# GpSimd's loads and normalisations in one pinned order, in a masked-patch loss on one core

## The chip, the core and the metric

The kernel runs on one core of a Trainium2 chip. The metric is the device time of one execution in microseconds (us), lower is better. The kernel before took 97.32 us in the median of three runs (97.21 to 97.70). The engines are called TensorE (PE, with its weight loads PEld), VectorE (DVE), ScalarE (ACT), GpSimd (POOL) and SyncE (SP), as in the profile.

## The reference

`pred` and `target` are float32 arrays of 32 x 147 x 768 (196 patches, three quarters of them masked). Each row of 768 values of the target is normalised, the squared difference to the prediction is averaged over the row, and the 147 rows of each batch entry are averaged.

```python
mean = target.mean(axis=-1, keepdims=True)
var = target.var(axis=-1, keepdims=True)
target = (target - mean) / np.sqrt(var + 1e-6)
loss = np.mean((pred - target) ** 2, axis=-1)
return loss.mean(axis=-1).astype(np.float32)
```

## The kernel before

The 4,704 rows are laid over 128 partitions: a batch entry has four partitions, and each of these has 37 rows of 768 values, save that the fourth has 36. So there are 36 full columns k = 0 to 35 of 128 rows, and a rest column 36 of 96 rows. Each tensor is loaded in pieces of columns. The target has a rest piece, whose tile is called t36, and nine pieces of four columns, t0, t4, ... t32 (the number is the first column). The prediction has p36, then p0, p4, ... p28 of four columns, and then p32 of two columns, p34 and p35 of one. All of them are loaded by GpSimd's DMA queue (line 66), which turns the float32 of the memory into bfloat16 on the way; a piece of four columns is 768 KB in the core's memory. Every piece has a buffer of its own, so no load waits for room. A load's issue does wait for something else: the loads take turns at eight completion semaphores, and a load is issued only when the eighth load ahead of it has landed.

For each target piece, `stats` takes mean and variance of each row on VectorE: two `bn_stats` of 384 values (line 116) and a `bn_aggr` (line 117) per column. ScalarE takes the square root for the piece (line 118, from `mv` to `r`), VectorE the reciprocal (line 120) and `nmr`, which is minus mean times `r`, by a `scalar_tensor_tensor` (line 121).

For each prediction piece, `losses` goes over its columns. GpSimd makes the normalised column `s` = t * r + nmr in bfloat16 (line 142, 128 x 768 each, 37 in all). TensorE forms pred - s in a PSUM tile `z` by four matmuls with the identity and minus the identity (line 147: `s` with 512 and 256 columns, then `p` with 512 and 256; I call these four a tile of TensorE's work). There are three `z` buffers. ScalarE squares `z` and sums it over the row (line 149, an ACTIVATE and an ACTIVATION_READ_ACCUMULATOR; "a Square" below is the pair). When all columns of a piece are squared, a small matmul adds the sums `rl` of the piece to `acc`, weighted by a mask (line 153, two of them in the trace). At the end VectorE adds four columns of `acc` (line 167), and SyncE writes 32 numbers out.

Each engine works through its own instructions in a fixed order. A scheduler sets that order when the kernel is built, from the code and its dependencies. On GpSimd it puts all 22 loads ahead of the first normalised column. `work`, the pool of `s`, has 6 buffers, and so has `small`, the pool of `r`, `nmr`, `mv`, `st` and `rl`.

Of the kernel before, what the change touches and what calls it, by code (L numbers as in the profile page):

```python
# [8 lines left out]
BF16 = mybir.dt.bfloat16  # L9
ALU = mybir.AluOpType  # L10
# [4 lines left out]
def kernel(  # L15
# [7 lines left out]
    nc = tc.nc  # L23
    B, N, D = pred.shape
    eps = 1e-6
    P = 128
    J = P // B
    KJ = (N + J - 1) // J
    KM = N - (J - 1) * KJ
    assert KJ == KM + 1  # L30
    RP = B * (J - 1)
# [6 lines left out]
    def main_rows(x, k0, k1):  # L38
        return bass.AP(tensor=x.tensor, offset=x.offset + k0 * D,
                       ap=[[N * D, B], [KJ * D, J], [1, (k1 - k0) * D]])  # L40

    def rest_rows(x):
        return bass.AP(tensor=x.tensor, offset=x.offset + KM * D,
                       ap=[[N * D, B], [KJ * D, J - 1], [1, D]])

    data = ctx.enter_context(tc.tile_pool(name="data", bufs=1))
    work = ctx.enter_context(tc.tile_pool(name="work", bufs=6))
    small = ctx.enter_context(tc.tile_pool(name="small", bufs=6))
    singles = ctx.enter_context(tc.tile_pool(name="singles", bufs=1))
    psum = ctx.enter_context(tc.tile_pool(name="psum", bufs=3, space=bass.MemoryType.PSUM))  # L50
# [3 lines left out]
    t_pieces = [None] + [(k, k + 4) for k in range(0, KM, 4)]  # L54
    p_pieces = [None] + [(k, k + 4) for k in range(0, KM - 4, 4)] + [(KM - 4, KM - 2), (KM - 2, KM - 1), (KM - 1, KM)]

    tbuf, pbuf = {}, {}

    def load(kind, piece):
        x = targ_f if kind == "t" else pred_f  # L60
        k0, k1 = piece if piece else (KM, KM + 1)
        rows = P if piece else RP
        dt = BF16 if kind == "t" else BF16
        til = data.tile([P, (k1 - k0) * D], dt, name=f"{kind}{k0}")
        eng = nc.gpsimd if kind == "t" else nc.gpsimd
        eng.dma_start(out=til[:rows], in_=main_rows(x, k0, k1) if piece else rest_rows(x))  # L66
        for k in range(k0, k1):
            (tbuf if kind == "t" else pbuf)[k] = (til, (k - k0) * D, rows)

    eps_t = singles.tile([P, 1], F32)  # L70
    nc.vector.memset(eps_t, eps)  # L71

    load("t", t_pieces[0])
    load("t", t_pieces[1])
    load("p", p_pieces[0])
    load("t", t_pieces[2])

    ident = singles.tile([P, P], BF16)
    nident = singles.tile([P, P], BF16)
# [12 lines left out]
        masks[name] = m  # L92

    seq = []
    for i in range(3, len(t_pieces)):
        seq += [("p", p_pieces[i - 2]), ("t", t_pieces[i])]
    seq += [("p", q) for q in p_pieces[len(t_pieces) - 2:]]
    for kind, piece in seq:
        load(kind, piece)

    acc = psum1.tile([B, 4], F32)
    rs = {}

    def stats(piece):
        k0, k1 = piece if piece else (KM, KM + 1)
        rows = P if piece else RP
        K = k1 - k0
        r = small.tile([P, K], F32, name="r")
        nmr = small.tile([P, K], F32, name="nmr")
        if norm_pix_loss:  # L110
            mv = small.tile([P, K, 2], F32, name="mv")
            for k in range(k0, k1):
                til, o, _ = tbuf[k]
                st = small.tile([P, 2, 6], F32, name="st")
                for j in range(2):
                    nc.vector.bn_stats(out=st[:rows, j, :], in_=til[:rows, o + j * half:o + (j + 1) * half])  # L116
                nc.vector.bn_aggr(out=mv[:rows, k - k0], in_=st[:rows])  # L117
            nc.scalar.activation(out=r[:rows], in_=mv[:rows, :, 1], func=ACTF.Sqrt,  # L118
                                 bias=eps_t[:rows], scale=1.0)
            nc.vector.reciprocal(out=r[:rows], in_=r[:rows])  # L120
            nc.vector.scalar_tensor_tensor(out=nmr[:rows], in0=mv[:rows, :, 0], scalar=-1.0,  # L121
                                           in1=r[:rows], op0=ALU.mult, op1=ALU.mult)
        else:
            nc.vector.memset(r, 1.0)
            nc.vector.memset(nmr, 0.0)
        for k in range(k0, k1):
            rs[k] = (r[:rows, k - k0:k - k0 + 1], nmr[:rows, k - k0:k - k0 + 1])

    n_acc = [0]
    total_acc = len(p_pieces)  # L130

    def losses(piece):
        k0, k1 = piece if piece else (KM, KM + 1)
        rows = P if piece else RP
        K = k1 - k0
        rl = small.tile([P, 4], F32, name="rl")
        for k in range(k0, k1):
            r, nmr = rs[k]
            til, o, _ = tbuf[k]
            ptil, po, _ = pbuf[k]  # L140
            s = work.tile([P, D], BF16, name="s")
            nc.gpsimd.tensor_scalar(out=s[:rows], in0=til[:rows, o:o + D], scalar1=r, scalar2=nmr,  # L142
                                    op0=ALU.mult, op1=ALU.add)
            z = psum.tile([P, 2 * BANK], F32, name="z")
            for src, so, w, first in ((s, 0, nident, True), (ptil, po, ident, False)):
                for c0, c1 in ((0, BANK), (BANK, D)):
                    nc.tensor.matmul(z[:rows, c0:c1], w[:rows, :rows], src[:rows, so + c0:so + c1],  # L147
                                     start=first, stop=not first)
            nc.scalar.activation(out=z[:rows, :D], in_=z[:rows, :D], func=ACTF.Square,  # L149
                                 accum_out=rl[:rows, k - k0:k - k0 + 1])  # L150
        if K < 4:
            nc.vector.memset(rl[:, K:], 0.0)
        nc.tensor.matmul(acc, masks["main" if piece else "rest"][:rows], rl[:rows],  # L153
                         start=n_acc[0] == 0, stop=n_acc[0] == total_acc - 1)
        n_acc[0] += 1

    done_p = 0
    cols = [p[1] if p else 0 for p in t_pieces]
    for i, tp in enumerate(t_pieces):
        stats(tp)  # L160
        hi = cols[i]
        while done_p < len(p_pieces) and (p_pieces[done_p] is None or p_pieces[done_p][1] <= hi):
            losses(p_pieces[done_p])
            done_p += 1

    ob = singles.tile([B, 1], F32)
    nc.vector.tensor_reduce(out=ob, in_=acc, axis=mybir.AxisListType.X, op=ALU.add)  # L167
# [36 lines left out]
```

## Time and profile before

| what | us |
|---|---|
| median of three runs | 97.32 |
| the profiled execution, its own time | 97.15 |
| its span, first to last instruction | 95.4 |
| GpSimd busy | 49.6 |
| VectorE busy | 43.9 |
| ScalarE busy | 36.1 |
| TensorE matmuls busy | 33.4 |

The profiled execution's time is 1.75 us longer than its span. The granted TensorE clock is 0.997. Rows of the timeline give the start, the duration, the engine, the line, the operation with output and inputs, the count of instructions merged in the row, and in brackets how long the engine was idle before and what ended the wait. Rows of 40 slices have one digit per fortieth of the span (2.39 us), the busy share in tenths.

### The profile page before, as it was taken

Reading aid. Unit: us, or ns where it says so; the run is one execution under the profiler, and the core shown is the slowest. Engines: PE = TensorE matmul, PEld = TensorE weight load, DVE = VectorE, ACT = ScalarE, POOL = GpSimd, SP = SyncE. Lnnn points to the kernel's source line nnn. Section 1 sums busy time; section 2 is a strip of 40 time slices with the busy share of each in tenths; the row PEclk is TensorE's granted clock in tenths of the full one; section 3 lists DMA queues with packets and bytes.
Section 4 is the critical chain, followed back from the end, with each engine's and each line's share of the span. In section 5 each row is a group of like instructions: output and inputs, shape, how many; then the busy total and the mean of one; then the engine's idle time right before and its main releaser. Section 6 shows DMA issues by size and latency. Waiting matters only on the chain.

```text
span 95.4 us, 762 instructions
## 1 busy us (share of the span) xinstructions
PE 33.4 (35%) x172; PEld 16.4 (17%) x172; DVE 43.9 (46%) x137; ACT 36.1 (38%) x85; POOL 49.6 (52%) x73
## 2 busy tenths in 40 slices
PE   0000000000000000000003999999897894388800
PEld 0000000000000000000002355444343442143400
DVE  0044989549439529629519609609980000100000
ACT  5010010100100100100001379999998999099910
POOL 5996220220220210211209999999999990899400
PEclk9999999999999999999999999999999999999998
DMA  0899999999999999999999999999990000000000
GB/s 0 142 211 211 211 214 214 211 211 214 221 217 209 214 216 216 219 211 211 219 216 214 211 211 219 219 212 211 204 165 0 0 0 0 0 0 0 0 0 0
DMA packets 3156, 14.49 MB, mean 152 GB/s; under 512 B 400, under 2 KB 848, under 8 KB 3152
## 3 DMA queue, kind: packets, MB, share of 16 engines
q0 software_dynamic: 3104, 14.45, 74.7%
q8 instruction: 1, 0.02, 0.1%
q14 instruction: 3, 0.02, 0.1%
q1 hardware_dynamic: 48, 0.00, 0.0%
HBM read 28.90 MB, written 0.00 MB: 303 GB/s over the span
## 4 chain that ended last, share of the span: by engine, by line
DMA 65%; ACT 15%; DVE 7%; issue 3%; POOL 3%; PE 2%; ACTq 0%; POOLq 0%
DMA t<-in_target_dram 65%; ACT z L149 14%; DVE st L116 4%; DVE nmr L121 3%; POOL s L142 2%; PE z L147 2%; POOL t L66 1%; DVE mv L117 1%; ACTq L149 0%; DVE r L120 0%; PE acc L153 0%; ACT r L118 0%; DVE ob L167 0%; POOLq L142 0%; ACTq L199 0%
## 5 line engine op out<-in xcount | busy, mean ns | idle before, releaser
L116 DVE BATCH_NORM_STATS2 st<-t 128x6 f32<-128x384 bf16 (+1 forms) x74 | 36.4, 531 | 25.2 <-DMA t<-in_target_dram 25.2
L147 PE MATMUL z<-s,nident 128*128 128x512 bf16 (+1 forms) x74 | 19.5, 347 | 56.2 <-POOL s L142 56.1
L142 POOL TENSOR_SCALAR s<-t,r,nmr 128x768 bf16<-128x768 bf16 (+1 forms) x37 | 35.8, 982 | 3.0 <-DVE r L120 2.9
L149 ACT ACTIVATE z<-z 128x768 f32<-128x768 f32 (+1 forms) x37 | 29.4, 794 | 5.0 <-PE z L147 3.9
L118 ACT ACTIVATE r<-mv,eps_t 128x4 f32<-128x4 f32 (+1 forms) x10 | 2.9, 295 | 49.2 <-DVE mv L117 35.8
L147 PE MATMUL z<-p,ident 128*128 128x512 bf16 (+1 forms) x74 | 19.7, 347 | 0.0
L66 POOL DMA_DIRECT2D p<-in_pred_dram x12 | 6.8, 566 | 22.4 <-DMA p<-in_pred_dram 16.2
L147 PEld LDWEIGHTS <-nident 128*128 128x128 bf16 (+1 forms) x74 | 7.2, 103 | 63.8 <-issue 54.3
L66 POOL DMA_DIRECT2D t<-in_target_dram x10 | 5.8, 584 | 14.0 <-DMA t<-in_target_dram 13.1
L147 PEld LDWEIGHTS <-ident 128*128 128x128 bf16 (+1 forms) x74 | 7.6, 103 | 5.6 <-issue 1.2
L117 DVE BATCH_NORM_AGGREGATE mv<-st 128x2 f32<-128x12 f32 (+1 forms) x37 | 7.3, 196 | 0.3
L149 ACT ACTIVATION_READ_ACCUMULATOR z<-z 128x1 f32 (+1 forms) x37 | 7.0, 190 | 0.0
L120 DVE RECIPROCAL r<-r 128x4 f32<-128x4 f32 (+1 forms) x10 | 1.7, 170 | 11.2 <-ACT r L118 11.2
L167 DVE TENSOR_REDUCE ob<-acc 32x1 f32<-32x4 f32 x1 | 0.1, 150 | 9.9 <-PE acc L153 9.9
L121 DVE SCALAR_TENSOR_TENSOR nmr<-mv,r 128x4 f32<-128x4 f32 (+1 forms) x10 | 3.7, 372 | 0.2
L153 PE MATMUL acc<-rl,mask_main 128*32 128x4 f32 x22 | 2.4, 183 | 1.8 <-ACT z L149 1.8
L153 PEld LDWEIGHTS acc<-rl,mask_main 128*32 128x32 f32 x22 | 1.5, 108 | 4.9 <-ACT z L149 3.3
L118 ACT ACT_TABLE_LOAD x1 | 1.3, 1283 | 0.8 <-PEq L185 0.8
L71 DVE MEMSET eps_t<- 128x1 f32 x1 | 0.1, 59 | 0.9 <-PEq L185 0.9
L82 POOL TENSOR_SCALAR_AFFINE_SELECT ident<-ident 128x128 bf16<-128x128 bf16 x1 | 0.4, 390 | 0.0
L82 POOL TENSOR_SCALAR_AFFINE_SELECT nident<-nident 128x128 bf16<-128x128 bf16 x1 | 0.4, 388 | 0.0
L90 POOL TENSOR_SCALAR_AFFINE_SELECT mask_main<-mask_main 128x32 f32<-128x32 f32 x1 | 0.3, 337 | 0.0
(14 smaller groups left out, 3.1 us busy)
## 6 DMA issues: line engine op xcount, KB each, us to landing
t<-in_target_dram POOLq DMA_DIRECT2D x9, 768.0 KB, 26.3
p<-in_pred_dram POOLq DMA_DIRECT2D x8, 768.0 KB, 29.0
p<-in_pred_dram POOLq DMA_DIRECT2D x1, 384.0 KB, 27.2
p<-in_pred_dram POOLq DMA_DIRECT2D x2, 192.0 KB, 23.1
t<-in_target_dram POOLq DMA_DIRECT2D x1, 144.0 KB, 3.2
p<-in_pred_dram POOLq DMA_DIRECT2D x1, 144.0 KB, 6.8
out_dram<-ob SPq DMA_DIRECT2D x1, 0.1 KB, 2.9
```

The lines of the kernel that those rows point to most:

```text
L66: eng.dma_start(out=til[:rows], in_=main_rows(x, k0, k1) if piece else rest_rows(x))
L82: nc.gpsimd.affine_select(out=til, in_=til, compare_op=ALU.not_equal, fill=v, base=0, pattern=[[-1, P]], channel_multiplier=1)
L90: nc.gpsimd.affine_select(out=m[:rows], in_=m[:rows], compare_op=ALU.is_ge, fill=0.0, base=per - 1, pattern=[[per, B]], channel_multiplier=-1)
L116: nc.vector.bn_stats(out=st[:rows, j, :], in_=til[:rows, o + j * half:o + (j + 1) * half])
L117: nc.vector.bn_aggr(out=mv[:rows, k - k0], in_=st[:rows])
L118: nc.scalar.activation(out=r[:rows], in_=mv[:rows, :, 1], func=ACTF.Sqrt, bias=eps_t[:rows], scale=1.0)
L120: nc.vector.reciprocal(out=r[:rows], in_=r[:rows])
L121: nc.vector.scalar_tensor_tensor(out=nmr[:rows], in0=mv[:rows, :, 0], scalar=-1.0, in1=r[:rows], op0=ALU.mult, op1=ALU.mult)
L142: nc.gpsimd.tensor_scalar(out=s[:rows], in0=til[:rows, o:o + D], scalar1=r, scalar2=nmr, op0=ALU.mult, op1=ALU.add)
L147: nc.tensor.matmul(z[:rows, c0:c1], w[:rows, :rows], src[:rows, so + c0:so + c1], start=first, stop=not first)
L149: nc.scalar.activation(out=z[:rows, :D], in_=z[:rows, :D], func=ACTF.Square, accum_out=rl[:rows, k - k0:k - k0 + 1])
L153: nc.tensor.matmul(acc, masks["main" if piece else "rest"][:rows], rl[:rows], start=n_acc[0] == 0, stop=n_acc[0] == total_acc - 1)
```

## The change

Normalising is taken out of `losses` into a function of its own, which writes `s` for all columns of a target piece as soon as their statistics are there, and which issues one load after the first column and one after the fourth. Loads and normalised columns carry a mark by which the scheduler keeps them in the order of the code. Three target pieces of four columns, not two, are loaded ahead of the first prediction piece of four columns, so each target piece from t8 on comes one place earlier among the loads and the prediction pieces p24 and p28 follow each other after t32. Eight loads come ahead of the first normalised column. The `work` pool has 20 buffers instead of 6. The last target piece gets its statistics and its normalised columns in two groups of two columns. `losses` of a prediction piece is now written after the normalising of the next target piece.

```diff
-    work = ctx.enter_context(tc.tile_pool(name="work", bufs=6))
+    work = ctx.enter_context(tc.tile_pool(name="work", bufs=20))
...
+    pin = tc.keep_in_program_order
...
-        eng.dma_start(out=til[:rows], in_=main_rows(x, k0, k1) if piece else rest_rows(x))
+        pin(eng.dma_start(out=til[:rows], in_=main_rows(x, k0, k1) if piece else rest_rows(x)))
...
     load("t", t_pieces[2])
+    load("t", t_pieces[3])
...
-    for i in range(3, len(t_pieces)):
-        seq += [("p", p_pieces[i - 2]), ("t", t_pieces[i])]
-    seq += [("p", q) for q in p_pieces[len(t_pieces) - 2:]]
-    for kind, piece in seq:
-        load(kind, piece)
+    for i in range(4, len(t_pieces)):
+        seq += [("p", p_pieces[i - 3]), ("t", t_pieces[i])]
+    seq += [("p", q) for q in p_pieces[len(t_pieces) - 3:]]
+    todo = iter(seq)
+
+    def load_next():
+        nxt = next(todo, None)
+        if nxt is not None:
+            load(*nxt)
+
+    for _ in range(3):
+        load_next()
...
+    sbuf = {}
+
+    def normalise(piece):
+        k0, k1 = piece if piece else (KM, KM + 1)
+        rows = P if piece else RP
+        for k in range(k0, k1):
+            r, nmr = rs[k]
+            til, o, _ = tbuf[k]
+            s = work.tile([P, D], BF16, name="s")
+            pin(nc.gpsimd.tensor_scalar(out=s[:rows], in0=til[:rows, o:o + D], scalar1=r, scalar2=nmr,
+                                        op0=ALU.mult, op1=ALU.add))
+            sbuf[k] = s
+            if k == k0 or k == k0 + 3:
+                load_next()
...
-            r, nmr = rs[k]
-            til, o, _ = tbuf[k]
+            s = sbuf[k]
             ptil, po, _ = pbuf[k]
-            s = work.tile([P, D], BF16, name="s")
-            nc.gpsimd.tensor_scalar(out=s[:rows], in0=til[:rows, o:o + D], scalar1=r, scalar2=nmr,
-                                    op0=ALU.mult, op1=ALU.add)
...
-    done_p = 0
-    cols = [p[1] if p else 0 for p in t_pieces]
-    for i, tp in enumerate(t_pieces):
-        stats(tp)
-        hi = cols[i]
-        while done_p < len(p_pieces) and (p_pieces[done_p] is None or p_pieces[done_p][1] <= hi):
-            losses(p_pieces[done_p])
-            done_p += 1
+    stats(t_pieces[0])
+    normalise(t_pieces[0])
+    for i, tp in enumerate(t_pieces[1:]):
+        k0, k1 = tp
+        groups = [tp] if i < len(t_pieces) - 2 else [(k0, k0 + 2), (k0 + 2, k1)]
+        for g in groups:
+            stats(g)
+            normalise(g)
+        losses(p_pieces[i])
+    for pp in p_pieces[len(t_pieces) - 1:]:
+        losses(pp)
```

The order of instructions shows what this moves. In the lists below a tile's name is followed by a number of its own (t4_81 is the tile t4), L66 and L67 are the loads, L142 and L147 on GpSimd are the normalised columns.

GpSimd before, its last six loads and the first columns:

```order
L66 DMA p24_125<-in_pred_dram 128x1x3072
L66 DMA t32_127<-in_target_dram 128x1x3072
L66 DMA p28_129<-in_pred_dram 128x1x3072
L66 DMA p32_131<-in_pred_dram 128x1x1536
L66 DMA p34_133<-in_pred_dram 128x1x768
L66 DMA p35_135<-in_pred_dram 128x1x768
L142 TENSOR_SCALAR s_149<-t36_75,r_138,nmr_139 96x768
L142 TENSOR_SCALAR s_182<-t0_77,r_159,nmr_160 128x768
```

GpSimd now, from the last of the eight loads that stand ahead of normalising:

```order
L67 DMA p4_107<-in_pred_dram 128x1x3072
L147 TENSOR_SCALAR s_120<-t36_75,r_110,nmr_111 96x768
L67 DMA t16_122<-in_target_dram 128x1x3072
L147 TENSOR_SCALAR s_146<-t0_77,r_124,nmr_125 128x768
L67 DMA p8_148<-in_pred_dram 128x1x3072
L147 TENSOR_SCALAR s_150<-t0_77,r_124,nmr_125 128x768
L147 TENSOR_SCALAR s_152<-t0_77,r_124,nmr_125 128x768
L147 TENSOR_SCALAR s_154<-t0_77,r_124,nmr_125 128x768
L67 DMA t20_156<-in_target_dram 128x1x3072
L147 TENSOR_SCALAR s_189<-t4_81,r_167,nmr_168 128x768
L67 DMA p12_191<-in_pred_dram 128x1x3072
```

Fourteen loads now stand behind one or more normalised columns; the last, p35, stands behind the first column of t24, and the load of t32 behind the fourth column of t12.

ScalarE before, around the square roots of the last two target pieces (L118 is a square root, L149 a Square; r_607 belongs to t32, z_520 to z_544 to p24, z_576 on to p28):

```order
L149 ACTIVATE z_528,rl_517<-z_528 128x768
L149 ACTIVATE z_536,rl_517<-z_536 128x768
L149 ACTIVATE z_544,rl_517<-z_544 128x768
L118 ACTIVATE r_551<-mv_553,eps_t_73 128x4
L118 ACTIVATE r_607<-mv_609,eps_t_73 128x4
L149 ACTIVATE z_576,rl_573<-z_576 128x768
```

ScalarE now, around the same roots (L127 is a square root, L169 a Square; r_525 belongs to t28, r_581 and r_599 to the two halves of t32, z_442 to z_460 to p16, z_500 is the first of p20):

```order
L127 ACTIVATE r_525<-mv_527,eps_t_73 128x4
L169 ACTIVATE z_442,rl_441<-z_442 128x768
L127 ACTIVATE r_581<-mv_583,eps_t_73 128x2
L169 ACTIVATE z_448,rl_441<-z_448 128x768
L169 ACTIVATE z_454,rl_441<-z_454 128x768
L169 ACTIVATE z_460,rl_441<-z_460 128x768
L127 ACTIVATE r_599<-mv_601,eps_t_73 128x2
L169 ACTIVATE z_500,rl_499<-z_500 128x768
```

Behind the root of t32 there stood 8 Squares; now 19 stand behind the root of its first half, and the last 16 of these, p20 to p35, behind the root of the second.

TensorE before, at the end of piece p20 (the rows of z_488 are the end of its fourth tile, those of z_520 the start of p24's first; the accumulating matmul of p20 comes only after two tiles of p24):

```order
L147 MATMUL z_488<-p20_121,ident_83 128x512
L147 LDWEIGHTS ident_83
L147 MATMUL z_488<-p20_121,ident_83 128x256
L147 LDWEIGHTS nident_84
L147 MATMUL z_520<-s_518,nident_84 128x512
```

TensorE now, at the end of piece p16 and the start of p20:

```order
L167 MATMUL z_460<-p16_251,ident_85 128x512
L167 LDWEIGHTS ident_85
L167 MATMUL z_460<-p16_251,ident_85 128x256
L173 MATMUL acc_109<-rl_441,mask_main_95 32x4
L167 LDWEIGHTS nident_86
L167 MATMUL z_500<-s_429,nident_86 128x512
```

The accumulating matmul of p16 now stands ahead of p20's first tile; that of p20 stands behind one tile of p24, that of p24 inside the second tile of p28, and that of p28 behind the two tiles of p32.

## The prediction

> **What bounds the kernel now.** I read the page's slices first, for where the time lies, then the timelines of GpSimd, ScalarE, VectorE and TensorE around the points where they wait. The page: the span and the slices of GpSimd and of the transfers.
>
> ```profile
> span 95.4 us, 762 instructions
> ...
> POOL 5996220220220210211209999999999990899400
> ...
> DMA  0899999999999999999999999999990000000000
> ```
>
> The transfers run without a gap through slice 30, that is to 71.6 us (30 x 95.4 / 40). GpSimd does next to nothing until the middle of the span and is then busy to the end. Its timeline says what it does there:
>
> ```profile
> 42.68 0.53 POOL L66 DMA_DIRECT2D p<-in_pred_dram  x1 [3.12 <-DMA t<-in_target_dram]
> 46.38 0.53 POOL L66 DMA_DIRECT2D p<-in_pred_dram  x1 [3.17 <-DMA p<-in_pred_dram]
> 50.00 0.53 POOL L66 DMA_DIRECT2D p<-in_pred_dram  x1 [3.10 <-DMA t<-in_target_dram]
> 50.57 20.27 POOL L142 TENSOR_SCALAR s<-t,r,nmr 96x768 bf16<-96x768 bf16 x21
> 71.05 7.74 POOL L142 TENSOR_SCALAR s<-t,r,nmr 128x768 bf16<-128x768 bf16 x8 [0.21 <-DVE r L120]
> 81.50 7.74 POOL L142 TENSOR_SCALAR s<-t,r,nmr 128x768 bf16<-128x768 bf16 x8 [2.71 <-DVE r L120]
> ```
>
> Each load waits about 3.1 us for an earlier one to land, and all 37 normalised columns stand behind the last load. So the first column starts at 50.57; 37 columns at 0.968 us (7.74 / 8) are 35.8 us, with 2.9 us of waits they end at 89.24. The timeline of ScalarE shows that it follows this pace:
>
> ```profile
> 55.44 0.30 ACT L118 ACTIVATE r<-mv,eps_t 128x4 f32<-128x4 f32 x1 [1.46 <-POOL s L142]
> 55.65 0.79 ACT L149 ACTIVATE z<-z 128x768 f32<-128x768 f32 x1
> ...
> 56.46 0.79 ACT L149 ACTIVATE z<-z 128x768 f32<-128x768 f32 x1
> ...
> 67.07 0.79 ACT L149 ACTIVATE z<-z 128x768 f32<-128x768 f32 x1
> ...
> 79.75 0.80 ACT L149 ACTIVATE z<-z 128x768 f32<-128x768 f32 x1
> 80.46 0.19 ACT L149 ACTIVATION_READ_ACCUMULATOR z<-z 128x1 f32 x1
> ...
> 83.45 0.80 ACT L149 ACTIVATE z<-z 128x768 f32<-128x768 f32 x1 [2.42 <-PE z L147]
> ...
> 90.20 0.80 ACT L149 ACTIVATE z<-z 128x768 f32<-128x768 f32 x1
> ```
>
> From 83.45 to 90.20 seven Squares take 0.964 us each: GpSimd's pace. From 56.46 to 67.07, with a stock of columns ready, thirteen take 0.816 us each: ScalarE's own pace. The last ACTIVATE ends at 91.00; 4.4 us later the span ends.
>
> **The loads move, the transfers should not.** GpSimd is now asked, per target piece, for 4 columns (3.87 us) and 2 issues (1.06 us), 4.93 us in all. The target pieces come as these rows of VectorE's timeline show, each the first statistics of a piece (t12, t28, t32), then the ends of t32's second and fourth aggregation and the `nmr` that follows:
>
> ```profile
> 27.78 1.48 DVE L116 BATCH_NORM_STATS2 st<-t 128x6 f32<-128x384 bf16 x3 [2.36 <-DMA t<-in_target_dram]
> ...
> 57.08 1.48 DVE L116 BATCH_NORM_STATS2 st<-t 128x6 f32<-128x384 bf16 x3 [3.10 <-DMA t<-in_target_dram]
> ...
> 64.40 1.48 DVE L116 BATCH_NORM_STATS2 st<-t 128x6 f32<-128x384 bf16 x3 [3.09 <-DMA t<-in_target_dram]
> ...
> 66.79 0.19 DVE L117 BATCH_NORM_AGGREGATE mv<-st 128x2 f32<-128x12 f32 x1
> ...
> 68.43 0.21 DVE L117 BATCH_NORM_AGGREGATE mv<-st 128x2 f32<-128x12 f32 x1
> 68.56 2.30 DVE L121 SCALAR_TENSOR_TENSOR nmr<-mv,r 128x4 f32<-128x4 f32 x1
> ```
>
> One period is 7.32 us, of two pieces of 3.66 us, so GpSimd has 2.4 us to spare in each. Each load issue now stands behind columns that wait for statistics. The load of t32 stands behind the fourth column of t12. t12 now comes one place earlier, at 24.1 (27.78 - 3.66); its statistics take 4.24 us (68.43 + 0.21 - 64.40), root and `nmr` another 0.5 or so, four columns and the issue between them 4.4: the load is issued at about 33.3, and t32's transfer can begin at 57.1, one piece ahead of its landing. The cover is 24 us, and the same count for p35, behind t24's first column, leaves about 18. So I cost the move at nothing for the transfers, with an end at 71.6 as before. Were the cover gone, every us of late issue would be a us of late end. That transfers slow down because GpSimd now normalises beside them is bounded by two stretches of the trace, without columns and with them, and by the last one, which holds the end of the data:
>
> ```profile
> 30.00:50.00 20.00, 0.00 (x0) 0.00 (x0) 11.32 (x36) 0.59 (x2) 2.64 (x5) 1.00 1.04 214
> 50.60:64.00 13.40, 12.38 (x58) 5.93 (x58) 7.54 (x23) 9.76 (x25) 13.40 (x14) 1.00 1.04 214
> 64.00:71.00 7.00, 6.09 (x33) 3.07 (x34) 6.56 (x16) 6.81 (x17) 6.84 (x8) 1.00 1.04 206
> ```
>
> The last figure is GB/s: 214 in both. I take no slowing; the far end is 206, 3.7% less, which would bring t32 2.2 us later.
>
> **What is late next.** With t28's columns done by about 62 (it comes at 53.4, 4.24 for statistics, 0.5, 3.9), GpSimd no longer holds anybody. The order on ScalarE does: 19 Squares stand behind the root of t32's first half, and 16 of them behind that of the second. These 16 (p20 to p35) would take 13.1 us at 0.816, and none may start before t32 has come, although p20 and its columns are there long before. The timelines of TensorE and of ScalarE have the rows that price the start of this run:
>
> ```profile
> 51.61 0.80 PE L147 MATMUL z<-s,nident 96*96 96x512 bf16 x2 [51.61 <-POOL s L142]
> ...
> 55.71 0.85 PE L147 MATMUL z<-s,nident 128*128 128x512 bf16 x2
> ...
> 56.99 0.61 PE L147 MATMUL z<-s,nident 128*128 128x512 bf16 x2
> ...
> 58.09 0.49 PE L147 MATMUL z<-p,ident 128*128 128x512 bf16 x2
> ...
> 58.74 0.49 PE L147 MATMUL z<-p,ident 128*128 128x512 bf16 x2
> ...
> 80.71 0.23 PE L153 MATMUL acc<-rl,mask_main 128*32 128x4 f32 x2 [1.05 <-ACT z L149]
> ...
> 82.54 0.48 PE L147 MATMUL z<-s,nident 128*128 128x512 bf16 x2 [1.61 <-POOL s L142]
> ```
>
> ```profile
> 53.08 0.79 ACT L149 ACTIVATE z<-z 96x768 f32<-96x768 f32 x1 [1.20 <-PE z L147]
> ```
>
> A tile of four matmuls takes 1.28 us (55.71 to 56.99) in TensorE's first 5.4 us of work, and 0.65 (58.09 to 58.74) after that. (The granted clock, the third figure from the end of the windows above, is 1.00 in both, so I go by the durations.) From a tile's first matmul to its Square is 1.47 us in the slow state (51.61 to 53.08) and 0.91 in the quick one (82.54 to 83.45).
>
> The sum, from t32's arrival. Statistics of t32 begin at 60.74 (64.40 - 3.66). Two columns take 2.58 (66.79 + 0.19 - 64.40): 63.32. Root and handover 0.25 (0.21 from 55.44 to 55.65, and a little for the semaphore): 63.57. Three Squares of p16, whose three `z` are ready, 2.45: 66.02. The second root falls here too, its statistics being ready at 64.98, and lies beside the next step. The accumulating matmul of p16 stands ahead of p20's first tile and waits for the Square: 0.96 from a Square's start to it (79.75 to 80.71) against a pace of 0.816 adds 0.15, its own work 0.22: p20's first tile starts at 66.39. Is TensorE slow there? Before that it works in pieces of at most three tiles, since the three `z` stay full until ScalarE's root lets them go: 3 x 1.28 = 3.8 us, short of the 5.4 that the trace needed. It also stands idle from about 60 to 66.4. The trace shows it quick after 1.61 us of idling and slow after 51.6, so both ends are open; I take slow, by the 5.4. First Square of p20: 66.39 + 1.47 = 67.86. Its fourth starts 3 x 1.28 later, 71.70. The accumulating matmul of p20 starts 0.96 after that and takes 0.22: 72.88, with p24's first Square beside it. p24's second tile reaches ScalarE 0.91 later, 73.79. From there 11 Squares at 0.816 are 8.98: 82.77. The later accumulations hide behind a Square each. p35 is in memory at 71.6, long before its turn. The end as before, 4.4: 87.17 of span. With the 1.75 us that lie around the span in the profiled execution it is 88.92 against its 97.15; the median is 0.17 above that execution, so I forecast **89.1 us**.
>
> The Trainium skill, TensorE: Matmul & The Clock Gate, Part 1, says the array runs at half rate by default and after an idle window of about 3.4 us, and at full rate after about 3.4 us of sustained work. The halves agree with 1.28 and 0.65, but the slow start here lasted 5.4 us; by 3.4 the sum would come out about 0.6 lower, at 88.5.
>
> **Small terms.** The extra root, reciprocal and `nmr` of the split piece cost 0.2 us each and lie beside Squares that are due anyway; the split lets the first root go 1.66 us earlier (4.24 - 2.58). Twenty buffers for `s` instead of six: columns from the 21st on reuse a buffer, each long read by then; in the trace no column waited for TensorE. The shared wait of roots on GpSimd (1.46 at 55.44) goes, since `r` is read early.
>
> **The rivals.** *TensorE is quick all through.* For it: 1.61 us of idling left it quick. Then p20's first Square starts at 67.30, its fourth at 69.75, p24's second at 71.84, and the end is 80.82 of Squares, 87.1 us. Chance 0.13. *TensorE stays slow to the end,* because it now works with pauses: 16 tiles of 1.28 from 66.39 and 1.0 for accumulations, then the last Square, 88.7; 95.0 us. Against it: from 83 on it worked 0.65 of every 0.96 us and stayed quick. Chance 0.04.
>
> *VectorE's `nmr` waits for GpSimd.* The one at 68.56 took 2.30 us and ended at 70.86, when the 21 columns in a row ended (50.57 + 20.27 = 70.84). GpSimd now normalises all along. If t28's `nmr` at 58.2 met a burst of 3.87 us, t32's statistics would start at 62.1 instead of 60.74: 90.5 us. Against it: t24's columns end near 55.5, so GpSimd would have to be 2.7 us late. The Trainium skill, GPSIMD Engine Reference, Specifications, says that GpSimd's ports to the memory are shared with VectorE, with contention where VectorE reads two inputs from it; `nmr` is such an instruction and the row agrees. Chance 0.06. *Transfers slower or t32 late,* by up to the 2.2 us above: 91.3 us. Chance 0.08.
>
> *ScalarE is not held by the roots,* if it could work p20's Squares before: the end would follow the last data, 71.6 + 0.91 + 0.82 + 4.4 + 1.75 + 0.17 = 79.7 us. The order of its instructions speaks against it. Chance 0.04.
>
> *GpSimd pays for every change between a load and a column,* and the kernel is slower than before. There are 14 loads among the columns, 28 changes. In the trace the one change, at 50.53, cost 0.04 us. The first `nmr`, that of t36, is there at 10.1:
>
> ```profile
> 9.97 0.14 DVE L121 SCALAR_TENSOR_TENSOR nmr<-mv,r 96x1 f32<-96x1 f32 x1
> ```
>
> From 10.2 37 columns and 14 issues of 0.53 are 43.2 us, to 53.4 if nothing ever waited. The columns would end as late as now, 89.24, from 1.28 us a change on; at 1.5 they end at 95.4 and the kernel takes 103.5 us. Chance 0.03. *The order does not hold on the chip,* and loads still go first: 97.3, no change. Chance 0.02.
>
> **How the numbers follow.** The forecast has 0.60. The range is **86.5 to 91.7 us**: it holds the quick TensorE (87.1), the late `nmr` (90.5) and the slower transfers (91.3), with 0.4 to 0.6 at each end for the small handovers that I rounded; 0.13 of the chances lie outside. About 0.5% is what a measurement of this kernel can tell from no change. Faster by more than that: all cases but the last two, **0.95**; within it **0.02**; slower **0.03**.
>
> **What would show it.** In the profile after: GpSimd's columns from about 10 us on, in groups of four with a load issue between; the transfers without a gap to about 71.6; t32's statistics at about 60.7; ScalarE idle for 4 to 5 us ahead of the root of t32's first half, then 19 Squares with few gaps, the largest ones at p20's slow tiles; the last ACTIVATE near 82.8. I would be wrong if the transfers showed gaps, if a load waited long behind a column, if GpSimd still ran columns after 70, or if ScalarE's idle time stood elsewhere than ahead of that root.

## The result and the profile after

The changed kernel took 89.42 us in the median of four runs (88.64 to 89.69), against 97.35 for the kernel before (97.21 to 97.70): the ratio is 0.9167, with a 95% interval of 0.9104 to 0.923. The forecast was 89.1 us, in a range of 86.5 to 91.7. The profiled execution took 89.54 us, with a span of 87.8.

The page after, span and slices (a slice is 2.2 us now):

```profile
span 87.8 us, 755 instructions
...
ACT  5010001010501940780492095050084678999900
POOL 4994332999999998398089469339428600000000
PEclk9999999999999955555589965579555569999995
DMA  0899999999999999999999999999999940000000
```

GpSimd's work now lies beside the transfers instead of behind them, and is over by slice 32. The transfers still run without a gap, to about 71 us. ScalarE, whose last Square ended at 91.0 before, still works to the end; in the last six of its busy slices TensorE, which feeds it, is the only engine that works beside it. GpSimd's timeline, at the start and the end of its columns:

```profile
10.18 0.98 POOL L147 TENSOR_SCALAR s<-t,r,nmr 96x768 bf16<-96x768 bf16 x1 [2.60 <-DVE nmr L130]
11.11 0.58 POOL L67 DMA_DIRECT2D t<-in_target_dram  x1
...
34.32 0.57 POOL L67 DMA_DIRECT2D t<-in_target_dram  x1
...
67.47 1.95 POOL L147 TENSOR_SCALAR s<-t,r,nmr 128x768 bf16<-128x768 bf16 x2 [0.31 <-DVE rl L172]
```

A load between two columns costs little more than a load cost before (0.57 to 0.58 us against 0.53), and t32's, the one at 34.32, is issued 27 us ahead of its landing. The chain that I had summed up can be read off VectorE, ScalarE and TensorE. VectorE, the arrivals of t28 and t32:

```profile
53.29 1.48 DVE L125 BATCH_NORM_STATS2 st<-t 128x6 f32<-128x384 bf16 x3 [2.25 <-DMA t<-in_target_dram]
...
61.28 1.48 DVE L125 BATCH_NORM_STATS2 st<-t 128x6 f32<-128x384 bf16 x3 [2.96 <-DMA t<-in_target_dram]
```

ScalarE: p16's first Square, the roots of t32's halves, and the Squares at which it waited:

```profile
58.01 0.80 ACT L169 ACTIVATE z<-z 128x768 f32<-128x768 f32 x1
...
63.95 0.29 ACT L127 ACTIVATE r<-mv,eps_t 128x2 f32<-128x2 f32 x1 [5.04 <-DVE mv L126]
64.15 0.79 ACT L169 ACTIVATE z<-z 128x768 f32<-128x768 f32 x1
...
66.60 0.28 ACT L127 ACTIVATE r<-mv,eps_t 128x2 f32<-128x2 f32 x1
68.50 0.80 ACT L169 ACTIVATE z<-z 128x768 f32<-128x768 f32 x1 [1.62 <-PE z L167]
...
72.14 0.80 ACT L169 ACTIVATE z<-z 128x768 f32<-128x768 f32 x1 [0.17 <-PE z L167]
...
74.17 0.80 ACT L169 ACTIVATE z<-z 128x768 f32<-128x768 f32 x1 [0.32 <-PE z L167]
...
82.32 0.79 ACT L169 ACTIVATE z<-z 128x768 f32<-128x768 f32 x1
```

TensorE, p16's last tile, the accumulation of p16 and p20's tiles, and the accumulation of p20:

```profile
58.96 0.50 PE L167 MATMUL z<-s,nident 128*128 128x512 bf16 x2 [0.76 <-ACT z L169]
...
66.75 0.27 PE L173 MATMUL acc<-rl,mask_main 128*32 128x4 f32 x2 [6.96 <-ACT z L169]
66.94 0.82 PE L167 MATMUL z<-s,nident 128*128 128x512 bf16 x2
...
68.20 0.85 PE L167 MATMUL z<-s,nident 128*128 128x512 bf16 x2
...
71.88 0.49 PE L167 MATMUL z<-s,nident 128*128 128x512 bf16 x2
...
73.09 0.23 PE L173 MATMUL acc<-rl,mask_main 128*32 128x4 f32 x2 [0.40 <-ACT z L169]
```

Between 58.91 and 63.95 ScalarE does nothing, although p20 has landed and its columns are made: the root of t32's first half stands in front of p16's last three Squares, and of all that follow. TensorE waits 6.96 us at the accumulation of p16, then takes 1.26 to 1.28 us for each of p20's first three tiles and 1.12 for the fourth, and the first Square behind the second root waits 1.62 us for it.

### The profile page after: what moved, and what is told of

It reads as the page before. It is cut to its first block, busy times and chain, and to the rows that moved or that the text cites. A ratio compares the mean times of both kernels' runs of the same rounds, so it can differ in the third digit from the quotient of the medians.

```text
span 87.8 us, 755 instructions
## 1 busy us (share of the span) xinstructions
PE 41.1 (47%) x172; PEld 18.4 (21%) x172; DVE 43.4 (49%) x139; ACT 35.3 (40%) x86; POOL 49.7 (57%) x73
## 4 chain that ended last, share of the span: by engine, by line
DMA 42%; POOL 18%; DVE 11%; ACT 9%; PE 7%; issue 6%; ACTq 1%; POOLq 0%
DMA t<-in_target_dram 42%; POOL s L147 13%; ACT z L169 9%; DVE st L125 9%; PE z L167 7%; POOL t L67 3%; POOL p L67 2%; DVE mv L126 1%; PE acc L173 1%; ACTq L222 1%; DVE nmr L130 1%; DVE r L129 0%; DVE ob L190 0%; ACTq L169 0%; ACT r L127 0%
## 5 line engine op out<-in xcount | busy, mean ns | idle before, releaser
L147 POOL TENSOR_SCALAR s<-t,r,nmr 128x768 bf16<-128x768 bf16 (+1 forms) x37 | 35.9, 977 | 18.6 <-DVE nmr L130 17.8
L167 PE MATMUL z<-s,nident 128*128 128x512 bf16 (+1 forms) x74 | 24.9, 429 | 17.9 <-POOL s L147 11.2
L169 ACT ACTIVATE z<-z 128x768 f32<-128x768 f32 (+1 forms) x37 | 29.3, 792 | 3.0 <-PE z L167 2.9
L167 PE MATMUL z<-p,ident 128*128 128x512 bf16 (+1 forms) x74 | 24.8, 426 | 0.0
L127 ACT ACTIVATE r<-mv,eps_t 128x4 f32<-128x4 f32 (+2 forms) x11 | 3.2, 295 | 44.2 <-DVE mv L126 44.2
L167 PEld LDWEIGHTS <-ident 128*128 128x128 bf16 (+1 forms) x74 | 9.4, 126 | 8.7 <-issue 5.4
L67 POOL DMA_DIRECT2D p<-in_pred_dram x12 | 6.9, 572 | 0.0
L169 ACT ACTIVATION_READ_ACCUMULATOR z<-z 128x1 f32 (+1 forms) x37 | 6.9, 185 | 0.0
L67 POOL DMA_DIRECT2D t<-in_target_dram x10 | 5.8, 595 | 0.8 <-POOLq L208 0.8
L129 DVE RECIPROCAL r<-r 128x4 f32<-128x4 f32 (+2 forms) x11 | 1.9, 172 | 3.5 <-ACT r L127 3.5
L130 DVE SCALAR_TENSOR_TENSOR nmr<-mv,r 128x4 f32<-128x4 f32 (+2 forms) x11 | 3.1, 282 | 0.2
```

Source lines behind the costliest of these rows:

```text
L67: pin(eng.dma_start(out=til[:rows], in_=main_rows(x, k0, k1) if piece else rest_rows(x)))
L147: pin(nc.gpsimd.tensor_scalar(out=s[:rows], in0=til[:rows, o:o + D], scalar1=r, scalar2=nmr, op0=ALU.mult, op1=ALU.add))
```

## The experiments

Two theories stood at the start. The first is the one of the forecast: GpSimd's late start is gone, and the end is now set by the Squares that ScalarE's fixed order leaves behind the roots of t32, with TensorE's slow start and the place of the accumulations. The second: the end follows t32's arrival, with a fixed length of work behind it, so that the earlier load and the earlier root of the split piece are what counts.

| run | what differs | us, median | ratio to before, 95% interval |
|---|---|---|---|
| changed kernel | | 89.42 | 0.917 (0.910 to 0.923) |
| order_only | kernel before, new order of loads | 97.59 | 0.998 (0.995 to 1.002) |
| two_ahead | old order of loads | 90.17 | 0.925 (0.918 to 0.932) |
| bufs6 | 6 buffers for columns | 89.44 | 0.917 (0.908 to 0.926) |
| one_group | t32 not split | 85.71 | 0.878 (0.871 to 0.885) |
| acc_late | accumulations last | 86.60 | 0.890 (0.884 to 0.895) |
| warm | TensorE kept at work | 87.67 | 0.900 (0.894 to 0.907) |
| five_ahead | five loads ahead | 84.06 | 0.860 (0.855 to 0.866) |
| five_one | five ahead, not split | 84.17 | 0.864 (0.861 to 0.868) |
| five_acc | five ahead, accumulations last | 83.50 | 0.857 (0.853 to 0.861) |
| pin_act | ScalarE's order pinned | 86.56 | 0.886 (0.880 to 0.892) |
| pin_both | VectorE's too | 87.07 | 0.894 (0.887 to 0.900) |
| pin_both_one | both pinned, not split | 83.06 | 0.851 (0.847 to 0.855) |

### The order of the loads, without the interleaving and with the old one

The kernel before with only the loads reordered (order_only):

```diff
     load("t", t_pieces[2])
+    load("t", t_pieces[3])
...
-    for i in range(3, len(t_pieces)):
-        seq += [("p", p_pieces[i - 2]), ("t", t_pieces[i])]
-    seq += [("p", q) for q in p_pieces[len(t_pieces) - 2:]]
+    for i in range(4, len(t_pieces)):
+        seq += [("p", p_pieces[i - 3]), ("t", t_pieces[i])]
+    seq += [("p", q) for q in p_pieces[len(t_pieces) - 3:]]
```

> The kernel before with only the order of the loads changed (three target pieces ahead); all loads still come ahead of all columns, the last piece is one group. Theory (GpSimd's columns, which start when the last load is issued, set the time of the kernel before): no change, 97.0 to 97.6 us. Rival (the earlier arrival of t32 is what the change gains): 3 to 4 us faster, about 93.7 us.

It measured 97.59 us, no change. t32 does come 3.8 us earlier, and GpSimd starts and ends its columns where it did:

```profile
50.42 20.29 POOL L143 TENSOR_SCALAR s<-t,r,nmr 96x768 bf16<-96x768 bf16 x21
...
81.37 7.74 POOL L143 TENSOR_SCALAR s<-t,r,nmr 128x768 bf16<-128x768 bf16 x8 [2.71 <-DVE r L121]
```

```profile
60.59 1.48 DVE L117 BATCH_NORM_STATS2 st<-t 128x6 f32<-128x384 bf16 x3 [3.10 <-DMA t<-in_target_dram]
```

The other way round, the changed kernel with the loads in the old order and the eight loads ahead of the columns kept (two_ahead):

```diff
-    load("t", t_pieces[3])
...
-    for i in range(4, len(t_pieces)):
-        seq += [("p", p_pieces[i - 3]), ("t", t_pieces[i])]
-    seq += [("p", q) for q in p_pieces[len(t_pieces) - 3:]]
+    for i in range(3, len(t_pieces)):
+        seq += [("p", p_pieces[i - 2]), ("t", t_pieces[i])]
+    seq += [("p", q) for q in p_pieces[len(t_pieces) - 2:]]
...
-    for _ in range(3):
+    for _ in range(4):
```

> The changed kernel with the loads in the order of before (two target pieces ahead of the first prediction piece), all else as changed; eight loads still come ahead of the first column. t32 now lands one piece (3.66 us) later, near 64.9. Theory (the Squares that stand behind the roots of t32, and TensorE's state when they start, set the end): here 16 Squares stand behind the first root and 15 behind the second, p16's four are done before, and the first three tiles of p20 are ready when the root comes; the Squares end near 82, a little earlier than 83.1, so about 88.4 us. Rival (the end is as far behind t32's arrival as in the changed kernel): 3.7 us later, about 93.1 us.

It measured 90.17 us: 0.75 above the changed kernel, within the spread of either, and between the two expectations. t32's statistics begin 3.9 us later (65.18 against 61.28), and the end moves by 0.75 us in the medians, by 1.2 in the two profiled executions: the second theory, which asks for all of the 3.9, falls. Mine missed 1.8 us. Its rows on TensorE, then on ScalarE:

```profile
69.02 0.50 PE L166 MATMUL z<-s,nident 128*128 128x512 bf16 x2 [1.17 <-ACT z L168]
...
70.90 0.82 PE L166 MATMUL z<-s,nident 128*128 128x512 bf16 x2 [1.06 <-ACT z L168]
...
72.74 0.82 PE L166 MATMUL z<-s,nident 128*128 128x512 bf16 x2
```

```profile
69.74 0.29 ACT L126 ACTIVATE r<-mv,eps_t 128x2 f32<-128x2 f32 x1 [0.78 <-DVE mv L125]
...
74.30 0.80 ACT L168 ACTIVATE z<-z 128x768 f32<-128x768 f32 x1 [0.93 <-PE z L166]
```

TensorE was quick at 69.02 (0.50 for the two matmuls) and slow again at 70.90 (0.82), after two pauses of little more than 1 us, and stayed slow for 6.5 us, to about 77.4. I had let its slow stretch begin once; it began twice.

### The place of the root: the last piece in one group

```diff
-        groups = [tp] if i < len(t_pieces) - 2 else [(k0, k0 + 2), (k0 + 2, k1)]
+        groups = [tp]
```

> The changed kernel with the last target piece in one group again. Its root can start only when all four columns have statistics, 1.6 us later, near 65.5. Theory: all four Squares of p16 now stand ahead of that root and fill the time in which ScalarE was idle, their accumulation is done by 61.5, and TensorE has three tiles of p20 ready; 16 Squares then follow the root with few gaps, ending near 80, so about 86.3 us, 3 us faster than with the split. Rival (the earlier root of the first half is what the split gains): 1.6 us slower than the changed kernel, about 91 us.

It measured 85.71 us (85.67 without its slowest execution), 3.7 us less than with the split. The profiled execution is that slowest one, at 86.68 us, so its rows are read for their order and their gaps. ScalarE ran so around the root of t32 (the first row is p16's last Square, the last one p35's):

```profile
60.49 0.80 ACT L169 ACTIVATE z<-z 128x768 f32<-128x768 f32 x1
...
65.62 0.30 ACT L127 ACTIVATE r<-mv,eps_t 128x4 f32<-128x4 f32 x1 [4.22 <-DVE mv L126]
65.82 0.79 ACT L169 ACTIVATE z<-z 128x768 f32<-128x768 f32 x1
...
79.36 0.79 ACT L169 ACTIVATE z<-z 128x768 f32<-128x768 f32 x1
```

The root comes 1.67 us later than the first one of the split did, and the end 3 us earlier, because the scheduler had put p16's last three Squares behind the split root and puts all four ahead of this one; with p16's accumulation done, three tiles of p20 are ready at 65.8, where the changed kernel's first came at 68.5. This is the order theory's case against the arrival theory, and it holds.

### TensorE's slow start and the accumulations

Fourteen matmuls on t32's raw columns, whose result nobody reads, ahead of p16's accumulation (warm); the rest of the work is the same:

```diff
+        if k0 == 16:
+            junk = psum1.tile([P, BANK], F32, name="junk")
+            t32 = tbuf[KM - 4][0]
+            for j in range(14):
+                pin(nc.tensor.matmul(junk, ident, t32[:, (j % 6) * BANK:(j % 6 + 1) * BANK],
+                                     start=True, stop=True))
```

> The changed kernel with 14 matmuls of 512 columns more, whose result nobody reads, on t32's raw columns, ahead of the accumulation of p16: TensorE works from t32's arrival, near 61.3, to about 66.6 and is quick when p20's first tile comes. Theory: p20's tiles take 0.65 us instead of 1.28 and the Squares end about 1.9 us earlier, about 87.5 us. Rival (TensorE's slow start is hidden or does not end by working): no change, or up to 0.4 us slower, 89.4 to 89.8 us.

It measured 87.67 us, 1.75 less than the changed kernel. TensorE works from t32's arrival on; p20's first tile then takes 0.66 us (66.99 to 67.65), and the first four Squares behind the second root follow each other in 0.81 us:

```profile
61.37 3.57 PE L177 MATMUL junk<-t,ident 128*128 128x512 bf16 x8 [1.00 <-DMA t<-in_target_dram]
...
66.99 0.50 PE L167 MATMUL z<-s,nident 128*128 128x512 bf16 x2
...
67.65 0.49 PE L167 MATMUL z<-s,nident 128*128 128x512 bf16 x2
```

More work on TensorE, less time: the slow start was on the path, and its price is near the one that the sum gave it (1.95 us between the quick and the slow case). Then all accumulations behind TensorE's last tile (acc_late):

```diff
-        rl = small.tile([P, 4], F32, name="rl")
+        rl = singles.tile([P, 4], F32, name=f"rl{k0}")
...
-        nc.tensor.matmul(acc, masks["main" if piece else "rest"][:rows], rl[:rows],
-                         start=n_acc[0] == 0, stop=n_acc[0] == total_acc - 1)
-        n_acc[0] += 1
+        late.append((masks["main" if piece else "rest"][:rows], rl[:rows]))
...
+    for j, (m, rl) in enumerate(late):
+        pin(nc.tensor.matmul(acc, m, rl, start=j == 0, stop=j == total_acc - 1))
```

> The changed kernel with all twelve accumulating matmuls moved behind the last tile of TensorE, each piece's sums in a buffer of its own. Nothing then holds p20's first tile until p16's last Square is done: TensorE can start it when the first z is free, near 65.0 instead of 66.9. Theory: its slow stretch starts 1.9 us earlier and the second gap, ahead of p24's second tile, goes too; the Squares end near 80.9 instead of 83.1, about 87.2 us. Rival (the accumulations hide behind Squares): no change, 89.4 us.

It measured 86.60 us, 2.8 less, 0.6 below what I expected; t32 came 0.7 us earlier in its profiled execution (60.57). p20's first tile starts right behind p16's second Square, and the first Square of p20 right behind the second root:

```profile
64.41 0.82 PE L167 MATMUL z<-s,nident 128*128 128x512 bf16 x2 [4.02 <-ACT z L169]
```

```profile
66.08 0.79 ACT L169 ACTIVATE z<-z 128x768 f32<-128x768 f32 x1
```

So matmuls of 0.2 us, in the wrong place of an engine's order, cost about as much as the slow start did: 2.8 us here against 1.75, but up to 0.7 of the 2.8 may be t32's earlier arrival, which pulls the first root with it (63.24 against 63.95).

### The cover of the loads, and the buffers

Five loads instead of eight ahead of the first column (five_ahead), so that each later one stands three places further back:

```diff
-    for _ in range(3):
+    for _ in range(0):
```

> The changed kernel with five loads instead of eight ahead of the first column, in the same order, so each of the other 17 stands three places later behind the columns; t32's load is issued near 44 instead of 34. The scheduler also moves ScalarE's roots: p20's Squares come before both roots of t32 and 12 are left behind them. By the cover worked out in the prediction the transfers do not notice: no gap, t32's statistics begin at 60.6 to 61.3 as in the changed kernel. Theory of the Squares: 12 instead of 16 behind the second root, about 85 us. Rival (the loads' place among the columns matters): gaps in the transfers, t32 and the end later, 90 us or more.

It measured 84.06 us. The load of t32 is issued at 45.14, 10.8 us later than in the changed kernel, and t32's statistics begin at 61.24, where they did: of the 24 us of cover 11 were given away and nothing moved. The gain comes from ScalarE: p20's four Squares now stand ahead of t32's roots and 12 behind them.

```profile
45.14 0.59 POOL L67 DMA_DIRECT2D t<-in_target_dram  x1
```

```profile
65.80 0.29 ACT L127 ACTIVATE r<-mv,eps_t 128x2 f32<-128x2 f32 x1 [1.59 <-DVE mv L126]
...
70.99 0.80 ACT L169 ACTIVATE z<-z 128x768 f32<-128x768 f32 x1 [0.91 <-PE z L167]
...
76.87 0.80 ACT L169 ACTIVATE z<-z 128x768 f32<-128x768 f32 x1
```

Six buffers for the columns instead of 20 (bufs6):

```diff
-    work = ctx.enter_context(tc.tile_pool(name="work", bufs=20))
+    work = ctx.enter_context(tc.tile_pool(name="work", bufs=6))
```

> The changed kernel with 6 buffers for the normalised columns instead of 20. GpSimd then waits for TensorE: columns of t24 and t28 are made only when p20's and p24's tiles are read, from 69 on, and those of t32 from about 75. All loads are issued by about 60, in time. Theory: the columns still come just ahead of TensorE's need, so no change or up to 1 us slower, 89.4 to 90.4 us. Rival (the 20 buffers carry the gain): GpSimd's columns fall behind the Squares as in the kernel before, 93 us or more.

It measured 89.44 us, no change, though GpSimd now waits 7.3 us for TensorE ahead of the column that it makes at 67.96:

```profile
67.96 0.99 POOL L147 TENSOR_SCALAR s<-t,r,nmr 128x768 bf16<-128x768 bf16 x1 [7.30 <-PE z L167]
```

Two more runs on the version with five loads ahead: with the last piece in one group (five_one, the edit of one_group on top), and with the accumulations last (five_acc, the edit of acc_late on top).

> The version with five loads ahead, with the last target piece in one group. p20's Squares stand ahead of t32's root in both, and 12 behind it. Theory (the split moved ScalarE's order in the changed kernel, and by that alone cost 3.7 us; the half piece itself is worth nothing): no change, 83.8 to 84.3 us. Rival (a split root is slow by itself): 2 to 4 us faster.

It measured 84.17 us, no change: where the Squares ahead of the root stay the same, the split neither costs nor gains.

> The version with five loads ahead, with the accumulating matmuls moved behind the last tile as well. In its trace ScalarE waited 0.9 us ahead of p28's first Square and 0.2 ahead of p32's, both behind an accumulation, and 0.55 at p24's slow tiles, which p24's landing starts. Theory: the first two go, the third stays: 1.0 us less, about 83.0 us. Rival (with 12 Squares left the end follows the transfers): no change, 84.1 us.

It measured 83.50 us, 0.56 less than five_ahead, where I expected about 1.0; the intervals of the two ratios overlap over more than half of their width, so the gain is not shown beyond doubt. The wait ahead of p28's first Square is gone, and one at p24's fourth tile, which was quick in the other trace, takes part of it back.

### Why pinning ScalarE's order was not enough

All roots and Squares in the order of the code (pin_act; `pin` around the two activations of `stats` and `losses`):

```diff
-            nc.scalar.activation(out=r[:rows], in_=mv[:rows, :, 1], func=ACTF.Sqrt,
-                                 bias=eps_t[:rows], scale=1.0)
+            pin(nc.scalar.activation(out=r[:rows], in_=mv[:rows, :, 1], func=ACTF.Sqrt,
+                                     bias=eps_t[:rows], scale=1.0))
```

> The changed kernel with ScalarE's roots and Squares pinned in the order of the code as well: p20's four Squares come before the root of t28, p24's four before the two roots of t32, and only 8 Squares (p28 to p35) are left behind those. Theory (the Squares behind t32's roots set the end): p24 lands near 64.9, its Squares run at TensorE's slow pace to about 70, roots to 70.7, then 8 Squares of 0.816 and about half a us of gaps; the last Square ends near 78, about 84.3 us. Rival (what stands behind t32's arrival is fixed work, and a later root only delays it): the roots of t32 come 5 us later than in the changed kernel, so 92 us or more.

It measured 86.56 us: 2.9 less than the changed kernel, 2.3 more than I expected. VectorE shows why. The root of t24 was done at 58, but its reciprocal stood behind the statistics of t32, which had not landed:

```profile
61.47 1.48 DVE L125 BATCH_NORM_STATS2 st<-t 128x6 f32<-128x384 bf16 x3 [3.69 <-DMA t<-in_target_dram]
...
65.62 0.12 DVE L129 RECIPROCAL r<-r 128x4 f32<-128x4 f32 x1
```

GpSimd made the columns of t24 from 66.15, and p24's first Square came at 68.49. So VectorE's statistics, reciprocals and `nmr` were pinned as well (pin_both; `pin` around the four instructions of `stats` on VectorE).

> The run with ScalarE's order pinned, with VectorE's statistics, reciprocals and nmr pinned in the order of the code too. There, the reciprocal of each piece stood behind the statistics of the next piece on VectorE, so GpSimd's columns came one piece late and TensorE waited for them. Theory: that is what the run of ScalarE's order alone missed; with the reciprocal ahead of the next statistics the columns of t24 are done by 60 and those of t28 by 67, and the last Square ends near 78, about 84.3 us. Rival (the roots that stand behind the Squares cost the 2 us, wherever the reciprocals stand): no change from that run, 86.6 us.

It measured 87.07 us: no better, as the rival had it. But the trace shows the first step done and a new wait in its place:

```profile
65.83 0.80 ACT L169 ACTIVATE z<-z 128x768 f32<-128x768 f32 x1 [3.13 <-PE z L167]
...
70.79 0.28 ACT L127 ACTIVATE r<-mv,eps_t 128x2 f32<-128x2 f32 x1
73.86 0.30 ACT L127 ACTIVATE r<-mv,eps_t 128x2 f32<-128x2 f32 x1 [2.79 <-DVE rl L172]
```

p24's first Square came at 65.83 as it should; then the pinned order held the statistics of t32's second half behind the `nmr` of its first, and ScalarE stood idle for 2.8 us between the two roots. With one group there is no second half (pin_both_one, the edit of one_group on top):

> The run with both orders pinned, with the last target piece in one group. In that run's trace the reciprocals ahead of the next statistics brought p24's first Square to 65.8 from 68.5, but the statistics of t32's second half then stood behind the nmr of its first half on VectorE, that nmr behind a root, and that root behind p24's Squares, so ScalarE waited 2.8 us ahead of the second root. Theory (that wait is all that hid the gain): with one group it goes, the one root follows p24's Squares near 70.8, 8 Squares follow from 71.1 and the last ends near 77.9, about 84.1 us. Rival (roots behind Squares are slow whatever the other engines do): 86.6 to 87.1 us as in the two runs before.

It measured 83.06 us, 1.0 below the expectation and the least of all runs, 0.851 of the kernel before (0.847 to 0.855; the interval of five_acc just touches it) and 6.4 us below the changed kernel. p24's first Square at 65.63, one root, 8 Squares behind it:

```profile
65.63 0.80 ACT L169 ACTIVATE z<-z 128x768 f32<-128x768 f32 x1 [2.84 <-PE z L167]
...
70.12 0.29 ACT L127 ACTIVATE r<-mv,eps_t 128x4 f32<-128x4 f32 x1
70.31 0.80 ACT L169 ACTIVATE z<-z 128x768 f32<-128x768 f32 x1
...
76.02 0.79 ACT L169 ACTIVATE z<-z 128x768 f32<-128x768 f32 x1
```

That VectorE's order has to be pinned for this is argued from the trace of pin_act; ScalarE's order pinned with one group, and VectorE's left to the scheduler, was not run.

## Why the prediction was right, step by step

| step | forecast | measured |
|---|---|---|
| first statistics of t32 | 60.74 | 61.28 |
| first Square behind its first root | 63.57 | 64.15 |
| first tile of p20 | 66.39 | 66.94 |
| first Square of p20 | 67.86 | 68.50 |
| fourth Square of p20 | 71.70 | 72.14 |
| second Square of p24 | 73.79 | 74.17 |
| last Square ends | 82.77 | 83.11 |
| from there to the end of the span | 4.4 | 4.7 |

**What bounded the kernel before** was right: loads moved without the interleaving changed nothing (order_only), and the gain stayed with the old order of loads (two_ahead, 7.2 us), with six buffers (bufs6) and without the split (one_group). No run takes back the interleaving alone. **The move at no cost for the transfers** was right, and five_ahead shows that 11 us of its cover could be given away. **What is late next** was right: ScalarE's idle time stood ahead of t32's first root, 5.04 us against 4 to 5, and 16 Squares followed the second root.

**TensorE slow at p20** was right, and its price nearly so (1.95 us in the sum, 1.75 in warm). But one of my two reasons failed: that pieces of three slow tiles, 3.8 us of work, are too short to make TensorE quick. After 4 us of work, from 54.21 to 58.20, it was quick at 58.96 (0.50 us for two matmuls). What the trace leaves is the other reason, the idle time ahead of p20, 6.96 us. The choice of slow was in part luck. The slow stretch was shorter than the 5.4 us of the trace before: p20's first tile began at 66.94, and the tile at 71.88 was quick, so at most 4.9.

**t32's arrival** was 0.54 us late. Of the nine other traces with this order of loads and VectorE's order left to the scheduler, six have it at 61.24 to 61.47 and three at 60.57 to 60.68, while t28 comes at 53.20 to 53.42 in all ten. One transfer tells them apart, which is none of the kernel's loads. The DMA view of the changed kernel for 57.9 to 59.1 us lists it (transfers, MB, share of the stretch):

```profile
q8 instruction: 1, 0.02, 4.9%
```

It has 16 KB and takes 0.94 us from 58.01. In the seven traces with a late t32 this transfer starts at 52.85 to 58.02, ahead of t32's landing; in the three others at 60.71 to 70.91, behind it. A load lands in 16 parts. In the changed kernel those of p20, the load ahead of t32, land within 0.75 us, and those of t32 within 1.41: the first comes on time (59.84 against 59.95 in acc_late), the last does not (61.25 against 60.55). No run moves this transfer alone, so that it delays t32 is likely, not shown.

The span was 0.63 us longer than forecast (87.8 against 87.17): t32's 0.54 had come down to 0.34 by the last Square, since p20's fourth tile was quicker than I took it, and the end behind the last Square was 0.3 longer. That the median is nearer, 0.3 off, is luck: I added 0.17 to the time of the profiled execution, and the median lies 0.12 below it.

**Wrong was one of the small terms.** I wrote that the split piece's root, reciprocal and `nmr` lie beside Squares that are due anyway, and that the split lets the first root go 1.66 us earlier. The root does go 1.67 us earlier than in one_group. But what it brought was the order in which three Squares of p16 stand behind that root, and with them p16's accumulation and p20's first tile: undone, the kernel is 3.7 us faster. The sum held this cost, since it was made from the order with the split in it; the sentence on the split alone was wrong. In the same way I counted the earlier arrival of t32 as the start of the whole chain, and with the old order of loads the end moves by 0.75 us only; in that trace fewer Squares stand behind t32's roots, and TensorE's slow stretch falls elsewhere.

**Accumulations** were priced where the order shows them, at 0.37 for p16's and 0.46 for p20's (73.79 against 71.70 + 2 x 0.816). That p16's also sets when TensorE can start at all, and so when its slow stretch begins, is what acc_late shows: p20's first tile at 64.41 instead of 66.94, of which 0.7 may go to t32.

Of the rivals, TensorE quick all through (87.1) is what the warm run made by hand, at 87.67. The `nmr` that waits for GpSimd did not meet a burst where it mattered: t28's, at 58.16, took 0.16 us; earlier ones took up to 0.73, with nothing waiting. The rival that ends slower, a price of every change between load and column, is excluded by the 0.04 to 0.06 us from the end of a load's issue to the next column.

## What to carry to other kernels

When an engine works in a fixed order, ask of each short instruction that waits for late data what stands behind it: here a root of 0.3 us held 19 Squares, seven of which (p16's last three and p20's four) had their loads landed and their columns made, and a matmul of 0.2 us held the next piece's first tile. A change that makes the last data arrive earlier, or split, is worth only what the order behind it lets through; compare the order with and without it before counting the gain. And when an order is pinned on one engine, look at the engines that feed it, instruction by instruction: here the wait moved first to one that was not pinned (pin_act), then to one whose pinned place came too late (pin_both).

## What the runs showed of the hardware

How long a pause makes TensorE slow does not come out as one number here. In the kernel before it stayed quick across pauses of 1.05 and 1.61 us with one accumulation of 0.23 us between them; in two_ahead it became slow after pauses of 1.17 and 1.06 with 0.8 us of work between them. So neither the longest pause nor the work of the last 3 us decides by itself. The Trainium skill, TensorE: Matmul & The Clock Gate, Part 1, has a free-running window of about 3.4 us for this. Slow stretches without a pause of 0.3 us or more lasted about 2.8 us (five_acc, from 57.02; two_ahead, from 64.28), 4.7 (changed kernel, from 66.94), 5.4 (kernel before, from 51.61), 6.0 (acc_late, from 64.41) and 6.5 (two_ahead, from 70.90), so one such window does not fit them all, and no run shows where a window begins.

The granted clock told the slow stretches of the changed kernel but not that of the kernel before. The stretches of the changed kernel in the table of windows, whose last figures are the granted clock, the transfers' share and GB/s:

```profile
30.00:50.00 20.00, 13.36 (x52) 5.63 (x50) 13.07 (x39) 9.01 (x24) 14.71 (x18) 0.66 1.05 216
64.00:71.00 7.00, 4.25 (x15) 2.12 (x16) 2.06 (x12) 4.69 (x12) 3.89 (x4) 0.50 1.04 204
```

It is 0.50 around p20's slow tiles of 1.26 to 1.28 us, while the kernel before showed 1.00 from 50.6 to 64 with tiles of 1.28 us in the first 5.4 us of it. And GpSimd's columns did not slow the transfers beside them: 216 GB/s with 14.71 us of GpSimd's work in 20, and 214 in the same stretch of the kernel before, where GpSimd made none.
